# Expert 1 at the fourth position, expert numbers ahead of the tables, logits on four column strips, and the left-over loop behind the last up product

## The chip, the cores and the metric

The kernel runs on one core of one Trainium2 chip. The core has a matrix engine (PE, with its own clock that a throttle grants), a vector engine (DVE), a scalar engine (ACT), GpSimd (POOL), a queue engine that issues most transfers (SP), and 16 DMA engines that carry them from the memory of the chip (HBM) to on-chip memory. The metric is the device time of one execution in microseconds, median of several.

## The reference

One decoder layer on 256 tokens of width 1024, in float32: two token mixers with gates, a layer norm, and a mixture of 32 experts, of which each token uses four, with a layer norm behind.

```python
    p = h @ w_in[l]
    ...
    h = layer_norm(DEEPNORM_ALPHA * h + merged @ w_out[l], ln_mix_g[l], ln_mix_b[l])
    f = moe_ffn(h, w_router[l], b_router[l], w_up[l], b_up[l], w_down[l], b_down[l])
    h = layer_norm(DEEPNORM_ALPHA * h + f, ln_ffn_g[l], ln_ffn_b[l])
```

The expert part, for an expert e and the tokens x that chose it:

```python
logits = (x @ w_router).astype(jnp.float32) + b_router.astype(jnp.float32)
top_val, top_idx = lax.top_k(logits, TOP_K)
gate = jax.nn.softmax(top_val, axis=-1)
...
gu = xe @ w_up[e] + b_up[e]
g = jnp.minimum(gu[:, :F], SWIGLU_LIMIT)
u = jnp.clip(gu[:, F:], -SWIGLU_LIMIT, SWIGLU_LIMIT)
act = (u + 1.0) * (g * jax.nn.sigmoid(SWIGLU_ALPHA * g))
return act @ w_down[e] + b_down[e]
```

Each expert has 8 MB of up weights and 4 MB of down weights.

## The kernel before

The first stage computes the mixers: products with weights split in a high and a low part (line 497), to 277 us. Its last product gives the residual `acc`; two layer norm statistics and `xn` (DVE, line 572) follow. Then comes the router: `turn_z` transposes `xn` in groups of four 128x128 blocks (line 939), `pick` multiplies with the router's weights (line 949) and finds the four best experts of each token on DVE (lines 951 to 962), two small products give each token its rank within an expert (lines 978 to 981), and `gather` picks an expert's tokens with one-hot matrices (line 611, evacuated by ACT at 619 and DVE at 616). `warm` issues products whose results nobody reads (line 931).

The second stage runs over 32 positions. A position takes an expert and has one, two or three blocks of 32 tokens; 52 blocks in all. Positions 0 and 1 are experts 0 and 1 by decree, the others are ordered by how many tokens chose the expert: `place_counts` ranks the experts, `place_left` counts tokens beyond the blocks, and `place_table` builds for every position the ranks, the gates and the expert's number (`ids`). A position's work is cut into steps a, b (the two halves of the up weights) and d (the down weights), in the order a0 b0 a1 d0 b1 a2 d1 b2 and so on. A step has two half slots of 2 MB; `up_part` issues the products of a half slot (line 652: eight products on four column strips of the array for a block), `down_half` those of a down half (line 679). Behind b come the swiglu (658 to 662), the transposes of its result (669) and of the gate weights (634), behind d the scatter into the sum `yacc` (694).

Weights stand in a ring of five buffers of 4 MB, ten half slots. `load_next`, called as soon as a half slot's products are issued, puts the next load of the list `order` into the queue of SP; SP issues its loads in order, and each waits until PE has read the slot. The expert's number comes into a register of SP (line 181) before its load. The first ten half slots are loaded during the mixer stage: up and down of position 0, up of position 1.

Tokens are gathered for several positions at once: a group holds up to four blocks (positions 0 and 1 are group 0), and its four gathers are dealt out between the products of the steps before, one for each `tick` of a quad, by the list `pend`; what is left of them is issued at once ahead of the a step that needs it.

Behind position 31's b and position 30's d stands a loop over blocks that did not fit (line 1049, `n_left` is zero here), then the last down product, the scatter, the statistics and the output. The two rows of the last norm are spread over partitions by four products (line 784), dealt out with `later`.

Of the kernel before, what the change touches and what calls it, by code (L numbers as in the profile page):

```python
# [7 lines left out]
FT = mybir.dt.float32  # L8
# [9 lines left out]
P = 128  # L18
D = 1024
# [8 lines left out]
WHOLE = range(4, 30)  # L28
RESIDUAL_AT, NORM_AT = (5, 11), 16
W1, W2, W3 = 3, 6, 4  # L30
# [5 lines left out]
SINGLE = (2, 3) + tuple(range(5, 24, 2)) + (27, 30, 31)  # L36
TRIPLE = (8, 14, 20)
N2, N3 = 15, 3
BLOCKS = [1 if p in SINGLE else 3 if p in TRIPLE else 2 for p in range(NE)]
CODES = [100, 101] + [0] * (NE - 2)  # L40
for blocks, lo in ((3, 0), (2, N3), (1, N2)):
    for i, p in enumerate([p for p in range(2, NE) if BLOCKS[p] == blocks]):
        CODES[p] = lo + i
assert sorted(CODES[2:]) == list(range(NE - 2))
# [10 lines left out]
def tile_kernel(ctx: ExitStack, tc: tile.TileContext, x, ln_in_g, ln_in_b, w_in, gmlp_ln_g, gmlp_ln_b,  # L55
# [37 lines left out]
    lnrow = keep.tile([2 * NC, P], FT, name="lnrow")  # L93
# [66 lines left out]
    expert_at = {0: 0, 1: 1}  # L160
# [48 lines left out]
    sp1 = s1.enter_context(tc.tile_pool(name="s1", bufs=1))  # L209
# [12 lines left out]
    acc = sp1.tile([P, T, D], FT, name="acc")  # L222
# [54 lines left out]
    def constants():  # L277
# [16 lines left out]
                       channel_multiplier=1, **iota)  # L294
        k["onesf"] = keep.tile([2 * NE, P], FT, name="onesf")
# [218 lines left out]
    for i in range(n_pieces):  # L514
# [8 lines left out]
        if i == 0:  # L523
            for t in range(T):
# [174 lines left out]
    ids = sp2.tile([P, NB], I32, name="ids")  # L699
    left = sp2.tile([P, 1], I32, name="left")  # L700
    e4 = sp2.tile([P, NE], FT, name="e4")
    fours = sp2.tile([P, 2], FT, name="fours")
    nc.gpsimd.iota(fours, pattern=[[4, 2]], base=0, channel_multiplier=0, allow_small_or_imprecise_dtypes=True)
    dyn["ids"] = ids
    cm = sp2.tile([NE, 16], FT, name="cm")
    keys = sp2.tile([NE, NE], FT, name="keys")
    perm = sp2.tile([NE, NB], FT, name="perm")
    shift = sp2.tile([NE, NB], FT, name="shift")
    nc.vector.memset(shift[:, :NE], 0.0)

    def place_counts():
        ps = ps_at()
# [4 lines left out]
        count, key, code, cap, over, nl = (cm[:, i:i + 1] for i in range(6))  # L717
# [7 lines left out]
        nc.vector.tensor_scalar(perm[:, :NE], const["code_of"], code, None, op0=OP.is_equal)  # L725

        nc.vector.tensor_scalar(cap, code, N2 - 0.5, 1.0, op0=OP.is_lt, op1=OP.add)
# [6 lines left out]
        nb = sp2.tile([NE, 1], BF, name="nb")  # L734
        nc.vector.tensor_copy(nb, nl)
        return nb

    def place_left(nb):
        ps = ps_at()
# [407 lines left out]
```

## Time and profile before

| | |
|---|---|
| median of 3 runs | 1248.02 us (1247.41 to 1249.36) |
| the profiled execution | 1248.0 us; its span 1246.3 us |
| PE busy | 1123.0 us, 90% |
| DVE busy | 414.9 us, 33% |
| bytes moved by DMA | 451.05 MB, mean 362 GB/s |
| mean granted clock of PE | 0.943 |

The page cuts the span in 40 slices; each digit is a busy share in tenths, and GB/s is what the DMA engines moved in a slice of 31 us:

```profile
PE   5999999998999899899988999887989889999884
...
DMA  9445546665899999999999999999999999999981
GB/s 356 172 141 197 202 161 251 263 269 211 334 383 399 429 432 421 435 428 431 423 429 430 427 428 432 427 429 431 430 429 428 428 430 428 425 431 426 426 368 52
```

A busy engine is not the same as a limit: PE counts as busy while a pipelined product waits for its operands. The span is from the first to the last instruction; the time of the run has 1.7 us more around it.

### The profile page before, as it was taken

Reading aid. Unit: us, or ns where it says so; the run is one execution under the profiler, and the core shown is the slowest. Engines: PE = TensorE matmul, PEld = TensorE weight load, DVE = VectorE, ACT = ScalarE, POOL = GpSimd, SP = SyncE. Lnnn points to the kernel's source line nnn. Section 1 sums busy time; section 2 is a strip of 40 time slices with the busy share of each in tenths; the row PEclk is TensorE's granted clock in tenths of the full one; section 3 lists DMA queues with packets and bytes.
Section 4 is the critical chain, followed back from the end, with each engine's and each line's share of the span. In section 5 each row is a group of like instructions: output and inputs, shape, how many; then the busy total and the mean of one; then the engine's idle time right before and its main releaser. Section 6 shows DMA issues by size and latency. Waiting matters only on the chain. (4 is left out here: it accounts for less than half of the span.)

```text
span 1246.3 us, 21719 instructions
## 1 busy us (share of the span) xinstructions
PE 1123.0 (90%) x9686; PEld 582.7 (47%) x9686; DVE 414.9 (33%) x784; ACT 214.8 (17%) x353; POOL 116.5 (9%) x125
## 2 busy tenths in 40 slices
PE   5999999998999899899988999887989889999884
PEld 4788788875443343434333444334334333433322
DVE  6854646564432222131223132221213122212213
ACT  3545553421110000101000001010101000100010
POOL 5700200000000000010001010000100000000000
PEclk9999999997999898899899999998989999999866
DMA  9445546665899999999999999999999999999981
GB/s 356 172 141 197 202 161 251 263 269 211 334 383 399 429 432 421 435 428 431 423 429 430 427 428 432 427 429 431 430 429 428 428 430 428 425 431 426 426 368 52
DMA packets 43903, 451.05 MB, mean 362 GB/s; under 512 B 2920, under 2 KB 3580, under 8 KB 26016
## 3 DMA queue, kind: packets, MB, share of 16 engines
q1 hardware_dynamic: 43776, 449.63, 86.7%
q8 instruction: 77, 1.26, 0.4%
q14 instruction: 18, 0.15, 0.0%
q10 hardware_dynamic: 32, 0.01, 0.0%
HBM read 448.58 MB, written 1.05 MB: 361 GB/s over the span
## 5 line engine op out<-in xcount | busy, mean ns | idle before, releaser
L652 PE MATMUL mm<-R,hT 128*32 128x512 f32 x3136 | 382.5, 613 | 19.3 <-DMA R<-in_w_up_dram 18.5
L679 PE MATMUL at<-R,actT 128*32 128x256 f32 x3328 | 225.9, 415 | 23.8 <-DMA R<-in_w_down_dram 9.9
L652 PEld LDWEIGHTS mm<-R,hT 128*32 128x32 f32 x3136 | 89.5, 111 | 206.6 <-issue 173.0
L658 DVE TENSOR_SCALAR gg<-mm 64x512 f32<-64x512 f32 x49 | 33.5, 683 | 401.1 <-PE mm L652 401.1
L679 PEld LDWEIGHTS at<-R,actT 128*32 128x32 f32 x3328 | 103.8, 118 | 123.0 <-issue 45.0
L661 POOL TENSOR_TENSOR gg<-gg,sg 64x512 f32<-64x512 f32 x52 | 66.1, 1271 | 860.3 <-ACT sg L659 842.9
L449 DVE TENSOR_TENSOR wlo<-R,whi 128x1024 fp32r<-128x1024 f32 x77 | 107.9, 1410 | 82.7 <-ACT whi L447 82.5
L497 PE MATMUL mm<-whi,hTl 128*128 128x512 f32 x256 | 101.6, 405 | 4.0 <-DVE hTl L269 4.0
L497 PE MATMUL mm<-wlo,hTh 128*128 128x512 f32 x256 | 101.4, 404 | 3.4 <-DVE wlo L449 3.4
L497 PE MATMUL mm<-whi,hTh 128*128 128x512 f32 x256 | 103.0, 411 | 0.0
L447 ACT ACTIVATE whi<-R 128x1024 fp32r<-128x1024 f32 x80 | 84.4, 1057 | 95.8 <-PE mm L497 93.0
L659 ACT ACTIVATE sg<-gg 64x512 f32<-64x512 f32 x52 | 32.8, 630 | 269.7 <-DVE gg L658 247.6
L686 ACT ACTIVATE y<-at 128x256 f32<-128x256 f32 x52 | 19.9, 383 | 331.7 <-PE at L679 331.7
L611 PEld LDWEIGHTS tp<-pt,xn 128*128 128x128 f32 x464 | 59.5, 201 | 33.3 <-DVE hT L616 22.1
L611 PE MATMUL tp<-pt,xn 128*128 128x128 f32 (+2 forms) x464 | 69.8, 296 | 0.0
L619 ACT ACTIVATE hT<-tp,lm 128x128 f32<-128x128 f32 (+2 forms) x58 | 25.7, 442 | 214.6 <-PE tp L611 214.6
L694 PE MATMUL ac<-y,qt 32*128 32x256 f32 x832 | 60.5, 405 | 0.5 <-ACT y L686 0.5
L671 DVE COPY actT<-tp 128x256 f32<-128x256 f32 x52 | 22.1, 425 | 109.0 <-PE tp L669 108.9
L497 PEld LDWEIGHTS mm<-wlo,hTh 128*128 128x128 f32 x256 | 49.0, 192 | 16.5 <-DVE wlo L449 5.1
L497 PEld LDWEIGHTS mm<-whi,hTl 128*128 128x128 f32 x256 | 48.8, 191 | 16.2 <-DVE hTl L269 5.1
L694 PEld LDWEIGHTS ac<-y,qt 32*128 32x128 f32 x832 | 38.1, 186 | 36.0 <-issue 33.7
L497 PEld LDWEIGHTS mm<-whi,hTh 128*128 128x128 f32 x256 | 49.0, 193 | 11.8 <-ACT hTh L266 0.9
(260 smaller groups left out, 821.8 us busy)
## 6 DMA issues: line engine op xcount, KB each, us to landing
R<-in_w_up_dram SPq DMA_DIRECT2D x52, 4096.0 KB, 38.7
R<-in_w_down_dram SPq DMA_DIRECT2D x26, 4096.0 KB, 33.6
R<-in_w_up_dram SPq DMA_DIRECT2D x24, 2048.0 KB, 8.5
R<-in_w_in_dram SPq DMA_DIRECT2D x13, 2048.0 KB, 9.0
R<-in_w_down_dram SPq DMA_DIRECT2D x11, 2048.0 KB, 10.5
R<-in_w_branch_a_dram SPq DMA_DIRECT2D x2, 2048.0 KB
R<-in_w_branch_b_dram SPq DMA_DIRECT2D x2, 2048.0 KB
R<-in_w_out_dram SPq DMA_DIRECT2D x2, 2048.0 KB
```

Source lines behind the costliest of these rows:

```text
L447: nc.scalar.activation(hi, w, AF.Copy)
L449: eng.tensor_tensor(lo, w, hi.bitcast(FT), op=OP.subtract)
L497: nc.tensor.matmul(ps[t], (a_l if k == 1 else a_h)[:, c, t * P:(t + 1) * P], (lo if k == 2 else hi)[:, cc], start=c == 0 and k == 0, stop= ...
L611: nc.tensor.matmul(ps[:, i * w:(i + 1) * w], zn[:, t, c * P:(c + 1) * P], pt[:, t, :w], start=t == 0, stop=t == T - 1)
L619: nc.scalar.activation(dst[:, c, :w], ps[:, i * w:(i + 1) * w], AF.Identity, scale=lm[:, 0, c:c + 1], bias=lm[:, 1, c:c + 1])
L652: nc.tensor.matmul(ps[n * CAP:(n + 1) * CAP], xs[:, c], w[:, o:o + 512], start=False, stop=c == NC - 1)
L658: nc.vector.tensor_scalar(gg, ps[:2 * CAP], LIMIT, None, op0=OP.min)
L659: nc.scalar.activation(sg, gg, AF.Sigmoid, scale=SW_ALPHA)
L661: nc.gpsimd.tensor_tensor(gg, gg, sg, op=OP.mult)
L671: nc.vector.tensor_copy(at, ps[:, :8 * CAP].rearrange("p (c h s) -> p c h s", c=4, h=2))
L679: nc.tensor.matmul(py[n * CAP:(n + 1) * CAP, :256], at[:, c, h], w[:, o:o + 256], start=h == 0 and c == 0, stop=h == 1 and c == 3)
L694: nc.tensor.matmul(to[n // 2][:, n % 2, t * 256:(t + 1) * 256], qt[s, t], y[s], start=start and t == 0, stop=stop and t == T - 1)
```

## The change

- Expert 1 moves from position 1 to position 3; the ten half slots loaded ahead are now up and down of position 0 and up of position 3. Positions 1 and 2 have one block each. Group 0 holds position 0 alone, group 1 positions 1 to 3.
- The table is cut in three: `place_counts` and `place_ids` give the numbers of the experts between the first up products; `first_table` gives ranks and gates of the positions; `place_caps` and `left_table` the left-over blocks, behind position 5.
- The row matrix of expert 0's bias is a constant made at the start; `acc` and `lnrow` live in the mixer's pool.
- The logits: the router's weights are now the standing operand, 32 columns on one of four strips of the array, and the transposed tokens the moving one, two products for each strip; ACT copies the result, and one more product with `stack` (four identity blocks) sums the strips and turns it.
- The gates are computed behind the first gathers; `warm` issues 4 and 2 products in place of 6 and 4.
- The loop over left-over blocks stands behind the last up product of position 31, ahead of its swiglu and of both last down products; the spreads of the last norm are issued at once behind position 30's b.

```diff
-WHOLE = range(4, 30)
-RESIDUAL_AT, NORM_AT = (5, 11), 16
-W1, W2, W3 = 3, 6, 4
+WHOLE = range(5, 30)
+LEFT_AT, RESIDUAL_AT, NORM_AT = 5, (7, 12), 17
+W1, W2, W3 = 3, 4, 2
...
+STATIC = {0: 0, 3: 1}
+SINGLE = (1, 2, 4, 6, 8, 10, 14, 16, 18, 20, 22, 25, 28, 30, 31)
...
-    order = [(p, k + h) for k, p in steps for h in "01"]
-    i = order.index((2, "a0"))
-    order[i:i + 4] = order[i + 2:i + 4] + order[i:i + 2]
+    uses = [(p, k) for k, p in steps]
+    heads = [(0, "a"), (0, "b"), (0, "d"), (3, "a"), (3, "b")]
+    order = [(p, k + h) for p, k in heads + [u for u in uses if u not in heads] for h in "01"]
...
+        nc.vector.tensor_scalar(rows0, k["rows"], 0.0, None, op0=OP.is_equal)
+
+        k["stack"] = keep.tile([P, NE], FT, name="stack")
+        nc.vector.tensor_copy(k["stack"], ident[:, :NE])
+        for n in range(1, 4):
+            nc.vector.tensor_tensor(k["stack"], k["stack"], ident[:, n * NE:(n + 1) * NE], op=OP.add)
...
+    def place_ids(ps):
+        at = ps[:, 512:512 + NE]
+        nc.tensor.matmul(at, iota_p[:NE].to_broadcast([NE, P]), perm[:, :NE], start=True, stop=True)
+        nc.vector.tensor_copy(ids, at)
+        nc.vector.tensor_scalar(e4, at, 4.0, None, op0=OP.mult)
...
-    groups = [[0, 1]]
-    for p in range(2, NE):
-        if p == 2 or sum(BLOCKS[q] for q in groups[-1]) + BLOCKS[p] > GRP:
+    groups = [[0]]
+    for p in range(1, NE):
+        if p == 1 or sum(BLOCKS[q] for q in groups[-1]) + BLOCKS[p] > GRP:
...
                 up_part([u], 3)
+                if u == LAST:
+                    left_blocks()
                 end_up(u)
...
+    def logits(t, ps):
+        for c in range(NC):
+            n = c % 4
+            nc.tensor.matmul(ps[n * NE:(n + 1) * NE, :P], wrg[:, c], hT2[:, c, t * P:(t + 1) * P], start=c < 4, stop=c >= 4)
+        lt = sp2.tile([P, T, P], FT, name="ptg", bufs=2)[:, 0]
+        nc.scalar.activation(lt, ps[:, :P], AF.Copy)
+        nc.tensor.matmul(ps[:, P:P + NE], lt, const["stack"], start=True, stop=True)
...
+    masks(0)
+    counts = place_counts()
     warm(W3, idle)
     gather_group(0, range(2))
+    start_up((0, 1))
+    first = [(0, 0), (0, 1)]
+    up_part(first[:1], 0)
+    place_ids(counts)
+    up_part(first[1:], 0)
+    gather_group(0, range(2, 4))
...
-                            later(1, lambda a=a, j=j: last_norm(a, j))
+                            last_norm(a, j)
```

The order on SP's queue, behind the last loads ahead of the router. R_69, R_70, R_68, R_67 and R_1944 (R_1951 now) are the five buffers; a row of 128x4096 is a half slot. Before:

```order
L203 DMA R_1944<-in_w_up_dram 128x4096 x2
L972 DMA tables<-in_b_down_dram 32x1024
L973 DMA tables<-in_ln_mix_b_dram 1x1024
L203 DMA R_69<-in_w_down_dram 128x4096 x2
L181 TENSOR_LOAD ids
```

And now:

```order
L206 DMA R_1951<-in_w_up_dram 128x4096 x2
L1036 DMA tables<-in_b_down_dram 32x1024
L1037 DMA tables<-in_ln_mix_b_dram 1x1024
L184 TENSOR_LOAD ids
L184 ISA x2
L206 ISA
L206 DMA R_69<-in_w_up_dram 128x4096
```

The load of an expert's number now stands ahead of the first load into a released slot, where expert 1's down weights, with a fixed number, stood.

The order on PE behind the last up products of position 0 (R_70), to position 1's up products and position 0's down products. `pt`, `xn` are a gather, `act` and `ptg` the transposes, `bup_h` the bias. Before:

```order
L652 MATMUL mm<-R_68,hT_1947 32x512 x4
L611 MATMUL tp<-pt,xn 128x128 x4
L679 MATMUL at<-R_67,actT 32x256 x8
L611 MATMUL tp<-pt,xn 128x128 x4
L679 MATMUL at<-R_67,actT 32x256 x8
L611 MATMUL tp<-pt,xn 128x128 x4
L679 MATMUL at<-R_67,actT 32x256 x8
L611 MATMUL tp<-pt,xn 128x128 x4
L679 MATMUL at<-R_67,actT 32x256 x24
```

And now:

```order
L660 MATMUL mm<-R_70,hT_1954 32x512 x20
L677 MATMUL tp<-ident,act 128x64 x8
L642 MATMUL tp<-ident,ptg 128x128 x4
L619 MATMUL tp<-pt,xn 128x128 x16
L653 MATMUL mm<-bup_h,rows 128x512
L654 MATMUL mm<-bup_l,rows 128x512
L660 MATMUL mm<-R_69,hT_1954 32x512 x4
L619 MATMUL tp<-pt,xn 128x128 x4
L660 MATMUL mm<-R_69,hT_1954 32x512 x4
L619 MATMUL tp<-pt,xn 128x128 x4
```

Group 1's gathers stand in one row ahead of position 1's first up product (R_69), where before they stood between the down products of position 0 (R_67); those of group 2 stand between position 1's up products.

The order on PE at the end. The rows of the loop's body are left out. Before:

```order
L679 MATMUL at<-R_1944,actT 32x256 x16
L669 MATMUL tp<-ident,act 128x64 x4
L634 MATMUL tp<-ident,ptg 128x128 x2
L694 MATMUL ac<-y,qt 128x256 x8
L1048 TENSOR_LOAD left
L1049 COMPARE_AND_BRANCH
...
L1049 UNCONDITIONAL_BRANCH
L679 MATMUL at<-R_70,actT 32x256 x32
L694 MATMUL ac<-y,qt 128x256 x8
```

And now:

```order
L660 MATMUL mm<-R_67,hT_1954 32x512 x8
L917 TENSOR_LOAD left
L918 COMPARE_AND_BRANCH
...
L918 UNCONDITIONAL_BRANCH
L687 MATMUL at<-R_69,actT 32x256 x32
L677 MATMUL tp<-ident,act 128x64 x4
L642 MATMUL tp<-ident,ptg 128x128 x2
L702 MATMUL ac<-y,qt 128x256 x8
L687 MATMUL at<-R_1951,actT 32x256 x32
L702 MATMUL ac<-y,qt 128x256 x8
```

Position 30's down product, its scatter and position 31's transposes have moved from ahead of the loop to behind it. The last branch of the loop carries waits for the eight load queues and for every engine, in both kernels.

## Rows read from the trace of the kernel before

**Rows 1.** The view of stretches: one row for each stretch of the span in us, with its length, the busy time of every engine (and its instructions), PE's granted clock, the busy share of the 16 DMA engines and GB/s.

```profile
core 0: us, PE busy (x) PEld busy (x) DVE busy (x) ACT busy (x) POOL busy (x), PEclk, DMA share, GB/s
360.00:380.00 20.00, 18.96 (x232) 10.62 (x228) 4.73 (x16) 2.60 (x6) 0.00 (x0) 1.00 0.93 384
380.00:400.00 20.00, 18.52 (x192) 7.16 (x188) 5.87 (x12) 1.64 (x3) 2.54 (x2) 1.00 0.98 418
1180.00:1197.00 17.00, 13.45 (x138) 4.57 (x134) 2.48 (x4) 1.01 (x2) 1.26 (x1) 0.98 1.01 428
...
1217.00:1219.00 2.00, 2.00 (x20) 0.92 (x12) 0.00 (x0) 0.38 (x1) 0.00 (x0) 0.50 0.20 80
1219.00:1220.00 1.00, 0.48 (x3) 0.30 (x3) 0.42 (x1) 0.00 (x1) 0.00 (x0) 0.50 0.00 0
1227.00:1230.40 3.40, 3.15 (x32) 1.54 (x36) 0.00 (x0) 0.00 (x0) 0.00 (x0) 0.50 0.00 0
1230.40:1236.00 5.60, 3.21 (x56) 1.60 (x48) 1.78 (x7) 0.38 (x1) 0.00 (x0) 1.00 0.00 0
```

**Rows 2.** The DMA view of 300 to 360 us: a bar of 40 slices of 1.5 us (tenths of the DMA engines' time), the bytes of the stretch, and the up loads issued in it with KB each and median us from issue to landing.

```profile
DMA  0007599999800999989899998994008799999999
...
DMA packets 1270, 18.64 MB, mean 311 GB/s; under 512 B 130, under 2 KB 130, under 8 KB 132
...
R<-in_w_up_dram SPq DMA_DIRECT2D x7, 2048.0 KB, 7.2
```

**Rows 3.** The timeline of SP's queue, 246 to 400 us: start, length, the line that issues, what is loaded, how many loads in the run.

```profile
304.66 3.78 SPq L203 DMA_DIRECT2D R<-in_w_down_dram  x2
318.70 2.13 SPq L203 DMA_DIRECT2D R<-in_w_up_dram  x2
...
328.55 19.47 SPq L203 DMA_DIRECT2D R<-in_w_up_dram  x4
```

**Rows 4.** The timeline of PE, 1160 us to the end: start, busy us, line, operation, out<-in with shapes, instruction records, and in brackets the idle time ahead of it with what ended it.

```profile
1170.01 6.50 PE L679 MATMUL at<-R,actT 128*32 128x256 f32 x64 [2.83 <-DMA R<-in_w_down_dram]
...
1201.31 2.07 PE L784 MATMUL tp<-tables,onesf 1*128 1x512 f32 x2
1203.31 1.94 PE L652 MATMUL mm<-R,hT 128*32 128x512 f32 x8
...
1214.91 3.64 PE L679 MATMUL at<-R,actT 128*32 128x256 f32 x32
1218.48 0.74 PE L669 MATMUL tp<-ident,act 64*128 64x64 f32 x4
...
1220.36 2.09 PE L694 MATMUL ac<-y,qt 32*128 32x256 f32 x16
1227.25 5.21 PE L679 MATMUL at<-R,actT 128*32 128x256 f32 x64 [4.80 <-issue]
```

**Rows 5.** The view of line 1049, the loop: the sequencers' instructions, count, durations in ns as least/median/most, first and last start.

```profile
L1049 PEldq EVENT_SEMAPHORE  x9: 51/51/51, 1222.5 to 1226.9; - x9
...
L1049 PEldq COMPARE_BRANCH  x3: 101/192/3354, 1221.1 to 1227.0; - x3
```

**Rows 6.** The timeline of PE from the mixer's last product to the first up product, columns as in rows 4.

```profile
283.21 0.80 PE L645 MATMUL mm<-bup_h,rows 128*128 128x512 f32 x1 [5.20 <-DVE rows L641]
...
288.13 0.75 PE L939 MATMUL ac<-ident,xn 128*128 128x128 f32 x4
288.71 1.87 PE L949 MATMUL ac<-wr,hT 128*128 128x32 f32 x16
290.96 2.85 PE L949 MATMUL ac<-wr,hT 128*128 128x32 f32 x16 [0.38 <-DVE lg L951]
...
300.86 1.92 PE L652 MATMUL mm<-R,hT 128*32 128x512 f32 x16
```

**Rows 7.** The timeline of DVE around the router, and of the last swiglu of the kernel, columns as in rows 4.

```profile
280.18 2.85 DVE L572 TENSOR_SCALAR xn<-acc,mv 128x1024 f32<-128x1024 f32 x2 [0.29 <-POOL mv L560]
...
295.13 0.29 DVE L962 TENSOR_REDUCE maskb<-eq 128x32 bf16<-128x128 f32 x1
...
1205.31 0.68 DVE L658 TENSOR_SCALAR gg<-mm 64x512 f32<-64x512 f32 x1 [6.23 <-PE mm L652]
...
1208.09 0.68 DVE L662 SCALAR_TENSOR_TENSOR act<-act,gg 64x512 f32<-64x512 f32 x1 [1.37 <-POOL gg L661]
```

**Rows 8.** The timeline of PE in the first expert, columns as in rows 4.

```profile
312.13 0.30 PE L757 MATMUL tp<-ident,gates 128*33 128x128 f32 x1
...
313.24 1.92 PE L652 MATMUL mm<-R,hT 128*32 128x512 f32 x16
315.09 0.43 PE L769 MATMUL at<-perm,tables 32*128 32x64 f32 x2
...
316.79 3.64 PE L652 MATMUL mm<-R,hT 128*32 128x512 f32 x32
...
323.46 0.47 PE L645 MATMUL mm<-bup_h,rows 128*128 128x512 f32 x1 [2.36 <-DVE act L660]
...
333.62 1.16 PE L611 MATMUL tp<-pt,xn 128*128 128x128 f32 x8
...
335.78 1.16 PE L611 MATMUL tp<-pt,xn 128*128 128x128 f32 x8
...
342.75 1.93 PE L679 MATMUL at<-R,actT 128*32 128x256 f32 x32 [0.50 <-ACT y L686]
```

More of the change, by code (lines that the diff above doesn't have):

```diff
@@ L523, in tile_kernel @@
         if i == 0:
+            acc = sp1.tile([P, T, D], FT, name="acc")
             for t in range(T):
@@ L716, in place_counts @@
             nc.tensor.matmul(ps[:NE, NE:NE + 1], maskb[:, t], ones[:, 0:1], start=t == 0, stop=t == T - 1)
-        count, key, code, cap, over, nl = (cm[:, i:i + 1] for i in range(6))
+        count, key, code = (cm[:, i:i + 1] for i in range(3))
         nc.vector.tensor_copy(count, ps[:NE, NE:NE + 1])
@@ L829, in col @@
     def col(p, t, what):
-        if p < 2:
-            return (rk, gates)[what][:, t, p:p + 1]
+        if p == 0:
+            return (rk, gates)[what][:, t, 0:1]
         return tab[:, what * T + t, p:p + 1]
@@ L893, in weigh, with left_blocks @@
         qts[u] = spread(weighted(lambda t: col(p, t, 0), lambda t: col(p, t, 1), k))
+    def left_blocks():
+        n_left = nc.values_load(left[0:1, 0:1], min_val=0, max_val=NOV)
+        with tc.For_i(0, n_left) as i:
+            cur = sp2.tile([P, 2 * T + 1, 1], FT, name="cur")
+            nc.vector.tensor_copy(cur, tab[:, :, bass.ds(i + NE, 1)])
+            idx = sp2.tile([P, 1], I32, name="idx")
+            nc.vector.tensor_copy(idx, cur[:, 2 * T])
+            e = nc.values_load(idx[0:1, 0:1], engines=[mybir.EngineType.SP], min_val=0, max_val=NE - 1)
+            up_e = wu[bass.ds(e, 1)].rearrange("o p n -> (o p) n")
+            ra, rbb, rd = [R[ring[NE - 1, k] // 2] for k in ("a0", "b0", "a0")]
+            nc.sync.dma_start(ra, up_e[:, 0:8192])
+            nc.sync.dma_start(rbb, up_e[:, 8192:16384])
+            four = sp2.tile([P, 1], FT, name="four")
+            nc.vector.tensor_scalar(four, cur[:, 2 * T], 4.0, None, op0=OP.mult)
+            pt = sp2.tile([P, T, GRP * CAP], FT, name="pt", bufs=2)
+            for t in range(T):
+                one_hot(pt[:, t, :CAP], CAP, cur[:, t])
+            xs = xT[(len(groups) - 1) % 2][:, :, :CAP]
+            gather(pt, xs, CAP)
+            ps = ps_mm()
+            up_bias(ps, bias_rows(four))
+            for c in range(NC):
+                up_quad(ps, (ra if c < 4 else rbb)[:, c // 2 % 2 * 4096:], xs, c)
+            nc.sync.dma_start(rd.rearrange("p (h n) -> p h n", h=2), wd[bass.ds(e, 1)].rearrange("o p h n -> (o p) h n"))
+            at = act_T(swiglu(ps))
+            qt = spread(weighted(lambda t: cur[:, t], lambda t: cur[:, T + t], 0))
+            py = ps_at()
+            for h in range(2):
+                down_half(py, at, rd[:, h * 4096:], h)
+            scatter(y_of(py), qt, yacc, False, False)
     def step(kind, p, free):
@@ L970, in tile_kernel @@
     both = ps_ac()
-    picks = [pick(t, both[:, t * 512:(t + 1) * 512]) for t in range(T)]
+    banks = [both[:, t * 512:(t + 1) * 512] for t in range(T)]
+    for t in range(T):
+        logits(t, banks[t])
+    picks = [pick(t, banks[t]) for t in range(T)]
     nc.sync.dma_start(bd[:NE], b_down[0])
     nc.sync.dma_start(bd[NE:], ln_mix_b)
-    idle = ps_ac()[:, :512]
+    idle = ps_at()
     warm(W2, idle)
     for t in range(T):
-        ps = picks[t][0][:, NE:2 * NE]
+        ps = banks[t][:, 256:256 + NE]
         nc.tensor.matmul(ps, before, maskb[:, t], start=True, stop=t == 0)
@@ L1006, in free @@
         def free(p, k):
-            if len(ring) < len(order) and order[len(ring)][0] > 1:
-                while place_table in [f for _, f in pend]:
-                    pend.pop(0)[1]()
             load_next(ring[p, k])
```

123 lines of the change are left out of this document (47 added, 76 removed).

## The prediction

> **What bounds the kernel now.** I read the strip of 40 slices on the page first: PE, the matrix engine, is 90% busy, but from slice 13 on DMA stands at 9 and GB/s between 421 and 435 until the last two slices. So the span has three stages with different limits, and each part of the change must be priced in its own.
>
> In the expert stage the stretches [rows 1] show a DMA share of 0.98 at 418 GB/s in 380 to 400 us and 1.01 at 428 in 1180 to 1197: the weight stream is the limit, and PE work there is free as long as slots come free in time. A 2 MB half slot takes 2.1 MB / 430 GB/s = 4.88 us of stream.
>
> Between the mixer's last product and the steady stream, the stream has holes. The bar of 1.5 us slices [rows 2] shows nothing from 300 to 304.5, nothing from 316.5 to 319.5, and a hole from about 341 to 345. Ten half slots were preloaded; the next six cross here. The SP queue, which issues every load, says why [rows 3]: 304.66 is the moment when PE releases the first slot, 318.70 the moment when the expert numbers exist. 18.64 MB in 60 us is 43.3 us of stream at 430 GB/s, so 16.7 us are lost, and 1.4 us more in 360 to 380 (share 0.93). Later nothing is lost.
>
> The tail begins when the last piece of the last down matrix lands: the share is 0.20 in 1217 to 1219 and 0.00 in the next microsecond [rows 1]. I call this moment L, about 1219.2. PE finishes expert position 30, then stands idle 4.80 us by "issue" before the last down product at 1227.25 [rows 4]; the line of the loop shows a single branch of 3354 ns on PE's sequencer [rows 5]. That is the loop over left-over blocks, whose body this input never enters. The end, 1246.3, is L + 27.1.
>
> So the time is: the moment the stream becomes continuous, plus bytes that do not change, plus the tail. Only the first and the last can move.
>
> **The front: expert numbers and first slots.** In before, the bias product waits until 283.21 for a DVE result [rows 6], because DVE makes the rows tile behind the two normalised halves, which it works on from 280.18 to 283.03 [rows 7]. With the rows made at the start, bias and warm-up run right behind the last product, and the transposes of the first half can start at 280.18 + 1.43 = 281.6; those of the second follow the second half, 283.0. In before the last of four groups ended at 288.88 (288.13 and 0.75 [rows 6]). At some 0.86 a group, the four end near 285.2: 3.7 us earlier.
>
> The logits then cost 1.87 and 2.85 us [rows 6] for two halves of eight products. For four strips of 128 columns there is no row. Bounds: an up part, also eight products on four strips but 512 columns wide, takes 1.92 us at full clock (16 records at 300.86 [rows 6]), so a quarter, 0.48, at best; 1.87 as in before at worst. To either come a copy by ACT (about 0.5, as a group's transposed copy costs) and one more product (about 0.3, as one of the table's). I take 1.0 + 0.5 + 0.3 a half. PE works in order, so the first logits stand at 285.2 + 1.8 = 287.0, the second at 288.8. The Trainium skill, "TensorE: Matmul & The Clock Gate", in the part on packing small matmuls, measured 2.38 times for three column strips; by that, as an estimate, 1.87 would become 0.8 and the sum fall by 0.4 us. No row of before shows it for this shape.
>
> In before the second mask was ready at 295.42, 1.6 us behind its logits (295.13 + 0.29 [rows 7], against 290.96 + 2.85 [rows 6]); now, with short waits, at 290.8. From there to the first up product it was 5.4 us (300.86). The gathers, the ranks and the masks between are the same, the products for the counts come in, four warm-up products go; I take 5.5: 296.3. The two parts of 1.92 us and the product for the numbers (0.2) end at 299.9: first slot free 4.8 us earlier than 304.66. The expert numbers are copied near 298.5, so SP, which waited for them until 318.70, does not wait here. Bounds for this moment: 297.5 if the clock stays full in the chain, 302.5 if half clock lasts through the first up parts, where 1.92 becomes 3.6.
>
> **The middle: where this gain goes.** Position 0 now is a group of its own, so positions 1 to 3 must be gathered before position 1's up products. In before those four gathers lay between the down quads of position 0, at 2.16 us a cycle (333.62, 335.78) [rows 8], and cost PE little that mattered. Now they stand alone, behind position 0's last up product. I build the new moments from the old durations: part 1 of both blocks behind the second gather pair, 299.9 + 2.0 + 3.7 = 305.6; position 0's gate half slots: 311.7 and, with 1.1 for the turned tables (312.13 to 313.24) and 1.3 for five of the seven products of the table (315.09 to 316.79) [rows 8], 315.3. Then PE waits for the second block's swiglu, 3.5 us from the end of its products (1205.31 to 1208.77 [rows 7]; the row at 323.46 shows PE idle 2.36 for it), and turns two activations and two weights, each with a copy: 322. Four gathers of 2.15: 330.5. Position 1's first half slot with two more gathers between its quads: 334.2; the second 338.5; position 0's down halves, at 1.93 for 32 records (342.75 [rows 8]), 346.0 and 349.
>
> Stream by these moments: a 2 MB load lands 7.2 us after its issue [rows 2], of which 4.88 are stream, so 2.2 pass first. Loads flow 302.1–307.0, 307.8–312.7, 313.9–318.8, 318.8–323.7, then nothing (all slots full) until 336.4, then to 341.3, to 346.2, and from 348.2 on without end. Lost in 300 to 360: 18.9 us, with six half slots carried before the hole closes, as in before. The same model on before's issues (304.66, 308.1, 318.7, 320.5, 328.55, 333.75, 344.74; [rows 3] has the first of each run) loses 17.7. So the change loses 1.2 more here, and spares up to 1.4 in 360 to 380, since position 3 lies preloaded and frees four half slots at once. End of the stream moves by −0.2 to +1.2; I take +0.3. The five microseconds gained at the front are spent waiting for the gathers.
>
> **The tail.** The four spreads of the last norm (about 2.07 us a pair of records at half clock [rows 4]) move ahead of position 31 and lie beside its loads. PE reaches the loop near 1203.4. The way out of the loop waits on the semaphores of all eight load queues on each engine, so PE, DVE, ACT and POOL now stand there until L, and both last down products stand behind it. The 3.35 us branch comes ahead of these waits and is hidden; what remains is the eight waits at 51 ns and a branch, some 0.9 us. Then: down of position 30, 64 records, 5.21 as the one at 1227.25 (half clock at its start, 3.2 us; [rows 1, 4]); act transposes and copy 1.2, weight transposes 0.44, scatter 1.15, down of position 31 at full clock 3.85 (twice the 1.93 at 342.75 [rows 8]; at half clock 32 records took 3.64 at 1214.91). The swiglu of position 31 (3.5) lies beside the first product. Sum: L + 0.9 + 5.2 + 1.2 + 0.4 + 1.2 + 3.9 = L + 12.8, against L + 13.3 in before (1227.25 + 5.21). The rest, 13.8 us, is the same. Tail: −0.5. If PE waits 5.2 us for its clock instead of 3.2, the first product takes 5.9: +0.2.
>
> Of the loop's three branches on PE the row has one at 101 ns, one at 192, one at 3354 [rows 5]. The Trainium skill, "Advanced Engine Details and Errata", under control flow timing, gives about 108 ns for a compare and branch; the trace agrees for one of three. By the page the move hides nothing and the tail stays as summed; by the row it matters which branch is the long one, and that is rival E.
>
> **At the start** DVE gets the stack (four operations of about 0.2) and the rows (0.27). They fall in its wait for x and for POOL; I take 0.1, at most 1.2.
>
> **Sum.** Profiled execution 1248.0 (span 1246.3 plus 1.7 outside), equal to the median 1248.02. 0.1 + 0.3 − 0.5 = −0.1: 1247.9. Two-tenths of a per cent, 2.5 us, is about what this measurement can tell from nothing.
>
> **The rivals.**
> A, faster: the front gain survives. If both evacuations of a gather overlap the next one's products and the clock is full in the chain, the first slot is free at 297.5 and position 1's at 330, and everything behind it starts 4 us earlier: 1243.8. For it: PE work of a gather is only 1.16 of 2.16. Against: one PSUM buffer, shown by the equal cycles.
> B, slower: the low clock lasts. PE stands 16 us in the loop instead of 4.8 and restarts cold. If the granted clock stays 0.50 through both products, they take 6.5 each (as the 64 records at 1170.01), scatter 2.09, transposes and copy 1.9 [rows 4]: 0.9 + 6.5 + 1.9 + 2.1 + 6.5 = L + 17.9, 4.6 more than before: 1252.9. It decides from the point at which the rise comes later than the first product's end. Against: the rise came 3.2 us after PE's restart in before.
> C, slower: the gathers standing alone run at half clock, since PE waits there by turns; each of the eight cycles grows by 1 us (1.16 of work becomes 2.2), of which the evacuation hides half: 4 us, 1251.9.
> E, slower: the long branch comes behind the waits in the new place, when the code behind the loop must still be brought in: +3.3, 1251.2. Against: in before it came ahead of them (4.80 idle, eight short waits last).
> D, faster: the loop's exit does not hold the down products. Then position 30's runs as its pieces land, and 31's ends some 3 us behind L: 10 us gained, 1238. Against: the same exit held PE in before.
>
> **Chances.** Forecast 0.48, A 0.22, B 0.11, C 0.10, E 0.05, D 0.04. The forecast's own range is 1245 to 1250.5. Faster: A, D and 0.04 of the forecast, 0.30; slower: B, C, E, 0.26; same 0.44. For eight in ten I leave out D and the far ends of B and C: 1243.0 to 1252.5.
>
> **What would show it.** First load of position 1 issued near 300; a hole in the stream from about 324 to 336; the four gathers in a row behind the weight transposes; PE idle in the loop from 1203 to L + 0.9; the branch hidden; first down product behind it 5 to 6 us. Wrong if the hole is shorter by 3 us, or if the clock row in the tail stays at 0.50.

## The result: slower by 0.6%

The changed kernel takes 1255.51 us (median of 7 runs, 1252.3 to 1257.9) against 1247.41 for the kernel before; the ratio is 1.0059, 95% interval 1.0045 to 1.0074. The prediction was 1247.9, between 1243.0 and 1252.5: the time lies outside the range, on the side that had 0.26. The profiled execution took 1257.9 us (span 1256.2), the longest of the seven, so sizes read from its trace are some 2 us above the median; another session gave 1257.06 (control, below).

### The profile after

Of the page, the strips of DMA and GB/s in 40 slices, now of 31.4 us:

```profile
DMA  9445556675499999999999999899999999999991
GB/s 372 152 162 182 193 194 252 257 294 213 168 400 430 437 431 430 424 432 431 432 431 429 393 425 392 365 430 431 432 430 436 431 429 428 434 431 428 429 414 58
```

Slice 11 (314 to 345 us) has 168 GB/s where before had 334, and slices 23 to 26, in the middle of the expert stage, have 393, 425, 392 and 365 where before had 427 to 432. These are two losses in two places, and both belong to the stream.

The first, in the DMA view of 300 to 360 us (bar of 1.5 us slices), beside which [rows 2] stands:

```profile
DMA  0079989999699999700000000000789999959899
...
DMA packets 1003, 14.80 MB, mean 247 GB/s; under 512 B 99, under 2 KB 99, under 8 KB 99
```

14.80 MB against 18.64: 3.84 MB less, at 430 GB/s 8.9 us. One long hole, from 325.5 to about 342, takes the place of the second and third short ones; the first, to 303, stays. Before lost 2.7 us of its own in 360 to 400 (384 and 418 GB/s, [rows 1]), which the change does not. So 6.2 us remain in this trace. By the bytes moved by 400 us, three other traces with the same front are 3.9 to 5.2 us behind before (control, second run of experiment 1, experiment 3), so the size changes from run to run.

SP's queue there: the first loads behind the router, and the fifth, which is position 2's first. The columns are those of [rows 3]:

```profile
302.36 5.86 SPq L206 DMA_DIRECT2D R<-in_w_up_dram  x2
```

```profile
341.80 4.64 SPq L206 DMA_DIRECT2D R<-in_w_up_dram  x2
```

And PE from the logits to position 1, which answers to [rows 6] and [rows 8]:

```profile
285.81 1.08 PE L1005 MATMUL ac<-hT,wr 128*32 128x128 f32 x16
...
297.17 2.95 PE L660 MATMUL mm<-R,hT 128*32 128x512 f32 x16
...
325.05 2.08 PE L619 MATMUL tp<-pt,xn 128*128 128x128 f32 x8 [0.52 <-DVE qt L644]
328.12 2.08 PE L619 MATMUL tp<-pt,xn 128*128 128x128 f32 x8 [0.99 <-DVE hT L624]
...
337.13 1.94 PE L660 MATMUL mm<-R,hT 128*32 128x512 f32 x8
```

The chain to the first up product is shorter, as summed (297.17, predicted 296.3), but that product runs largely at the low clock (2.95 instead of 1.92 us), and the four gathers of group 1 take 3.07 us each from start to start, not 2.15: their products take 2.08 instead of 1.16 [rows 8], and PE waits 0.99 for the evacuation before each next one.

The stretches, columns as in [rows 1]:

```profile
317.00:325.00 8.00, 3.08 (x16) 1.69 (x12) 4.82 (x12) 0.63 (x1) 2.69 (x2) 0.67 1.01 432
325.00:336.00 11.00, 7.96 (x32) 7.08 (x33) 1.74 (x5) 1.37 (x3) 0.00 (x0) 0.50 0.00 1
...
360.00:380.00 20.00, 15.28 (x162) 5.82 (x154) 4.77 (x10) 1.42 (x3) 1.27 (x1) 1.00 1.01 429
380.00:400.00 20.00, 19.63 (x212) 7.60 (x216) 3.21 (x9) 0.61 (x3) 1.27 (x1) 1.00 1.01 430
700.00:720.00 20.00, 20.00 (x194) 8.10 (x190) 5.10 (x9) 1.65 (x3) 1.46 (x2) 1.00 0.91 371
720.00:740.00 20.00, 17.56 (x228) 8.03 (x216) 5.32 (x13) 0.82 (x3) 1.09 (x1) 1.00 0.98 419
740.00:760.00 20.00, 16.80 (x144) 9.82 (x148) 5.07 (x15) 2.68 (x6) 1.25 (x1) 0.83 1.02 439
760.00:780.00 20.00, 20.00 (x186) 5.91 (x178) 3.87 (x6) 1.26 (x2) 2.44 (x2) 1.00 0.92 377
780.00:800.00 20.00, 17.43 (x210) 8.53 (x210) 6.51 (x17) 1.40 (x3) 1.40 (x2) 0.91 1.00 415
800.00:820.00 20.00, 19.04 (x198) 7.57 (x186) 3.83 (x9) 1.44 (x3) 1.27 (x1) 1.00 0.79 324
...
1225.00:1229.00 4.00, 0.00 (x0) 0.00 (x0) 0.00 (x0) 0.00 (x0) 0.00 (x0) 0.50 0.44 178
1229.00:1230.00 1.00, 0.00 (x0) 0.00 (x0) 0.00 (x0) 0.00 (x0) 0.00 (x0) 0.50 0.00 0
```

In 325 to 336 the clock is at 0.50 throughout and next to nothing moves (1 GB/s). In 700 to 820 the DMA share is under one in slices where PE is busy 20.00 of 20.00. That alone does not make PE the limit, but SP's loads do: those issued from 690 to 810 us whose landing the trace has land 12.0 to 19.3 us after their issue, where in before they take 36.5 to 39.4. A whole load of 4 MB is 9.8 us of stream at 430 GB/s, so there is hardly a load in hand: SP issues one only when PE frees a slot. The missing shares of the six slices add up to 7.6 us; in bytes, as the first loss was counted, it is more: 391 GB/s in 700 to 820 where 430 could pass, 10.9 us. The last bytes land at about 1229.3, ten us later than before.

The tail, on PE, which answers to [rows 4], and the long branch of the loop, which answers to [rows 5]:

```profile
1212.16 1.92 PE L660 MATMUL mm<-R,hT 128*32 128x512 f32 x16
1230.32 5.71 PE L687 MATMUL at<-R,actT 128*32 128x256 f32 x64 [16.24 <-issue]
...
1238.62 3.66 PE L687 MATMUL at<-R,actT 128*32 128x256 f32 x64
```

```profile
L918 PEldq COMPARE_BRANCH  x3: 101/192/5887, 1212.9 to 1230.1; - x3
```

PE stands in the loop for 16.24 us, leaves it 1.0 us behind the last landing and runs the two down products. From the last landing to the end of the span it is 26.9 us (before 27.1). The branch grew to 5.89 us and is hidden under the wait.

### The profile page after: what moved, and what is told of

It is laid out like the page before. It is cut to its first block, busy times and chain, and to the rows that moved or that the text cites. A ratio compares the mean times of both kernels' runs of the same rounds, so it can differ in the third digit from the quotient of the medians.

```text
span 1256.2 us, 21756 instructions
## 1 busy us (share of the span) xinstructions
PE 1117.4 (89%) x9698; PEld 584.3 (47%) x9698; DVE 414.1 (33%) x788; ACT 215.2 (17%) x355; POOL 116.4 (9%) x124
## 4 chain that ended last, share of the span: by engine, by line
PE 70%; DMA 19%; DVE 7%; ACT 2%; POOL 2%; issue 1%; ACTq 0%; DVEq 0%; SPq 0%; POOLq 0%
PE mm L660 22%; PE mm L504 15%; PE at L687 13%; DMA R<-in_w_up_dram 10%; DMA R<-in_w_down_dram 8%; PE tp L619 5%; PE ac L702 4%; PE tp L677 2%; PE at L660 2%; PE tp L642 1%; DVE wlo L456 1%; PE mm L653 1%; DVE gg L666 1%; POOL gg L669 1%; DVE act L668 1%
## 5 line engine op out<-in xcount | busy, mean ns | idle before, releaser
L687 PE MATMUL at<-R,actT 128*32 128x256 f32 x3328 | 216.6, 403 | 30.0 <-issue 16.2
L619 PEld LDWEIGHTS tp<-pt,xn 128*128 128x128 f32 x464 | 63.3, 212 | 37.1 <-DVE hT L624 24.7
L619 PE MATMUL tp<-pt,xn 128*128 128x128 f32 (+2 forms) x464 | 74.1, 308 | 3.5 <-DVE hT L624 3.0
L677 PEld LDWEIGHTS tp<-ident,act 64*128 64x128 f32 x208 | 28.8, 209 | 57.4 <-issue 23.0
```

Source lines behind the costliest of these rows:

```text
L619: nc.tensor.matmul(ps[:, i * w:(i + 1) * w], zn[:, t, c * P:(c + 1) * P], pt[:, t, :w], start=t == 0, stop=t == T - 1)
L677: nc.tensor.transpose(ps[:, c * 2 * CAP:(c + 1) * 2 * CAP], v[:, c], ident[:2 * CAP, :2 * CAP])
L687: nc.tensor.matmul(py[n * CAP:(n + 1) * CAP, :256], at[:, c, h], w[:, o:o + 256], start=h == 0 and c == 0, stop=h == 1 and c == 3)
```

## The experiments

Twelve runs, in three sessions of four: the numbered experiments 1 to 4; the control, the repairs, the second run of 1 and the loop; and the last four. In each the kernel before ran too (1247.17, 1246.01 and 1247.23 us); ratios are to it.

**1. One block list.** The places of one-block and two-block positions:

```diff
-SINGLE = (1, 2, 4, 6, 8, 10, 14, 16, 18, 20, 22, 25, 28, 30, 31)
+SINGLE = (1, 2, 4, 6, 8, 10, 12, 14, 16, 18, 20, 22, 25, 30, 31)
```

> The changed kernel with one list altered: position 12 gets one block and position 28 two (in the changed kernel 12 has two and 28 one), so one-block and two-block positions alternate from 4 to 19. Theory 1 (the row of two-block positions 11 to 13 with a three-block position 15 behind makes PE the limit in the middle): the DMA share of 700 to 820 us goes back from 0.91, 0.98, 1.02, 0.92, 1.00, 0.79 to about 1.00 in each 20 us, the wait from issue to landing of a 4 MB load there grows from 12 to 19 us to over 20, and the time falls by 3 to 8 us, to about 1250. Rival (a disturbance of that one profiled execution, or the later hole at the start): the time stays at 1255 and the middle is again uneven.

Measured: 1247.54 us, ratio 1.0006 (0.9997 to 1.0015). Most of the loss is gone by one number moved in a list. It ran once more for a trace that can be read:

> The kernel with position 12 at one block and 28 at two once more, for its trace. Theory 1: the time is 1247 to 1248 again; the DMA share in 700 to 820 is about 1.00 throughout, while the hole behind 324 stays and the load of position 2 goes out near 338 to 342. Rival: the middle still dips, and the gain lies in a shorter hole.

Measured: 1247.9 us, ratio 1.0015 (1.0006 to 1.0025). The stretches of this second trace:

```profile
325.00:336.00 11.00, 8.02 (x34) 5.97 (x34) 2.52 (x9) 1.84 (x4) 0.00 (x0) 0.50 0.00 0
700.00:720.00 20.00, 16.55 (x216) 7.90 (x212) 4.89 (x12) 1.40 (x3) 0.44 (x2) 1.00 1.01 431
760.00:780.00 20.00, 17.43 (x205) 8.34 (x201) 4.85 (x14) 0.77 (x2) 0.62 (x1) 0.83 0.99 426
800.00:820.00 20.00, 20.00 (x206) 8.98 (x206) 6.93 (x15) 2.95 (x6) 2.56 (x2) 1.00 1.02 435
```

The hole is still there, as expected: nothing moves in 325 to 336, and the first load of position 2 goes out at 339.69. The dip in the middle is gone, 1.01, 0.99 and 1.02 where it was 0.91, 0.92 and 0.79. PE even has slack in two of the three, and the loads issued from 690 to 810 land after 22.4 to 35.8 us. In the changed kernel positions 11, 12 and 13 have two blocks each, a part of the residual (eight small products and a spread) falls at 12, and position 15 has three blocks. From the first bias product of position 11 to that of 16 (617.2 to 778.6 us) PE is busy 150.3 us; the loads of five positions, 30 half slots of 4.88, are 146.4. In this trace, with position 12 at one block, the same stretch (615.0 to 756.9) has 132.8 us of PE. So the work of PE is longer than its loads there, and the slots that the stream had in hand run out. Theory 1 holds.

**2. Two banks for the gathers.**

```diff
-        gather(pts[g], xT[g % 2], width[g], js, g == 0)
+        gather(pts[g], xT[g % 2], width[g], js, g < 2)
```

> The changed kernel with group 1's gathers using two PSUM banks by turns, as group 0's do. Theory 2 (the four gathers standing alone ahead of position 1, at half clock and with one bank, lengthen the hole in the stream): the cycle of 3.07 us falls to about 2.1, the load issued at 341.8 goes out near 338, the time falls by 3 to 4 us, to about 1251.5. Rival (the hole is set by the swiglu of position 0 and the slots, whatever the gathers take): the issue stays near 341 and the time at 1255.

Measured: 1248.49 us, ratio 1.0011 (1.0001 to 1.0022). PE in the hole, and the stretch of 325 to 336 with two of the middle:

```profile
322.59 1.91 PE L619 MATMUL at<-pt,xn 128*128 128x128 f32 x8
324.30 1.25 PE L619 MATMUL tp<-pt,xn 128*128 128x128 f32 x8
325.50 1.16 PE L619 MATMUL at<-pt,xn 128*128 128x128 f32 x8
326.54 1.16 PE L619 MATMUL tp<-pt,xn 128*128 128x128 f32 x8
```

```profile
325.00:336.00 11.00, 11.00 (x83) 6.49 (x83) 3.71 (x12) 2.74 (x6) 0.00 (x0) 1.00 0.35 127
760.00:780.00 20.00, 18.44 (x152) 6.51 (x148) 10.07 (x22) 1.89 (x3) 3.83 (x3) 0.97 0.97 384
780.00:800.00 20.00, 18.98 (x270) 9.10 (x262) 0.54 (x3) 1.15 (x3) 0.00 (x0) 0.95 0.79 326
```

The second bank does more than expected: without the wait for each evacuation PE works without a break, the clock rises during the second gather (1.00 in 325 to 336), and the cycle falls from 3.07 to 1.7, 1.2 and 1.0. In the four traces with one bank for these gathers the clock of 325 to 336 is 0.50, in the two with two banks 1.00 and 0.76. The load of position 2 goes out at 331.30 instead of 341.80; 19.29 MB move in 300 to 360. Of these 10.5 us the edit does not make 1.75, by which the first load was already earlier (300.61); the second run of experiment 1, with one bank and its first load at 300.22, sent position 2's at 339.69. The time falls by 7 us against the first session's 1255.51. The dip in the middle stays (0.79 in 780 to 800): the two losses are separate. Theory 2 holds, with a larger size.

**3. The loop at its old place** in the changed kernel.

```diff
                 up_part([u], 3)
-                if u == LAST:
-                    left_blocks()
...
-                            last_norm(a, j)
+                            later(1, lambda a=a, j=j: last_norm(a, j))
         while pend:
             pend.pop(0)[1]()
+    left_blocks()
```

> The changed kernel with the left-over loop at its old place (behind position 30's down product) and the four spreads of the last norm dealt out as before. Theory 3 (the move of the loop is worth nothing, as the sum of the prediction had it): from the last landing to the end 27 us as in both kernels, time 1255 within 1.5. Rival (PE standing 16 us in the loop and restarting at half clock costs several us): the time falls by 3 us or more.

Measured: 1250.69 us (1246.72 to 1257.75, 12 runs), ratio 1.0040 (1.0019 to 1.0060). Neither: the runs lie in heaps near 1247, 1250 and 1256. The profiled one (1249.91) has a tail of 27.7 us from the last landing, as theory 3 has it, but less of a dip in the middle (shares of 0.96 and more; 419 GB/s in 700 to 820, against 391 in the changed kernel and 385 in its control, which have the same program up to there). What changed between its runs can't be read from one trace, so this run decides nothing on the loop. It suggests that the size of the dip changes with the run: the stream there is on the edge.

**4. The old places under the new front.** Expert 1 at position 1 again, with the groups, blocks and whole loads of the kernel before; constant rows, strips, early numbers and the moved loop stay.

```diff
-STATIC = {0: 0, 3: 1}
+STATIC = {0: 0, 1: 1}
...
-heads = [(0, "a"), (0, "b"), (0, "d"), (3, "a"), (3, "b")]
+heads = [(0, "a"), (0, "b"), (0, "d"), (1, "a"), (1, "b")]
...
-    groups = [[0]]
+    groups = [[0, 1]]
```

> The changed kernel with expert 1 at position 1 again, group 0 holding positions 0 and 1, and the blocks and whole loads of the kernel before; the new front (constant rows, strips, early expert numbers) and the moved loop stay. Theories 1 and 2 together (the new places cost, the front does not): no gathers ahead of position 1, the hole behind 324 us gone, no loss in the middle, time 1243 to 1247. Rival (the front itself costs): 1250 or more.

Measured: 1235.76 us, ratio 0.9913 (0.9900 to 0.9927): 11 us faster than before, beyond what was expected. The DMA view of 300 to 360 us:

```profile
DMA  8998998979999998999898105698999999999999
...
DMA packets 1506, 22.05 MB, mean 368 GB/s; under 512 B 160, under 2 KB 160, under 8 KB 160
```

22.05 MB against 18.64 in before and 14.80 in the changed kernel. The bar shows one hole of two slices, at 333. So the front, which I had thought to be spent on waiting, is worth 3.4 MB, 7.9 us of stream, when no gathers stand ahead of position 1. The new places cost all of that and more.

**Control and repairs.** The changed kernel once more, in the second session:

> The changed kernel itself once more, beside the others of this call. If its loss is its own and not that of the first session: 1252 to 1258 again, with the hole behind 324 us and the dip of the DMA share between 700 and 820. If the first session was disturbed: 1247 to 1250, as the kernels with one part altered showed, and then each of those gains has to be measured anew.

Measured: 1257.06 us, ratio 1.0079 (1.0052 to 1.0105), with 15.24 MB in 300 to 360, and shares of 0.86, 0.96 and 0.74 in 700 to 720, 760 to 780 and 800 to 820. The loss is the kernel's own. Then three repairs at once, the lists of experiment 1, the banks of 2, and this:

```diff
-            while kind == "a" and j_of[group_of[p]]:
-                pend.pop(0)[1]()
...
+    def need(p, j):
+        g = group_of[p]
+        while j_of[g] and j_of[g][0] <= j:
+            pend.pop(0)[1]()
```

`need(p, i)` stands ahead of each half slot's products.

> The changed kernel with three repairs: position 12 at one block and 28 at two, group 1's gathers on two PSUM banks, and each gather issued only ahead of the up products that read it and not all four ahead of position 1. Theories 1 and 2 (two independent losses, about 6 us and 2 to 8 us): both gone, 1236 to 1241. Rival (the two gains are the same microseconds, since a stream that starts earlier only meets the slow middle earlier): 1246 to 1248.

Measured: 1242.41 us, ratio 0.9965 (0.9950 to 0.9980), 14.6 us below the control: close to the sum of the two gains (9 us below the control in the second run of 1; 7 in experiment 2, by the first session), and a little above the range expected. So the two losses are not the same microseconds. The gathers issued late were no help: two run wholly or mostly at half clock again (1.92 and 1.78 us), the load of position 2 goes out at 331.79, no earlier than in experiment 2, and 17.53 MB move, 1.76 fewer than there. Repaired, the change is faster than before by 0.35%, yet 7 us behind the old places.

**The loop again,** under the old places (the edit is that of experiment 3):

> The kernel with the old places and the new front, with the loop and the spreads of the last norm put back as well. Theory 3 (the move of the loop is worth half a microsecond): 1235.5 to 1237, from the last landing to the end 27 us. Rival (the move gained several us of the 12): 1238 or more; or it cost some: 1233 or less.

Measured: 1231.97 us, ratio 0.9893 (0.9875 to 0.9912), 3.8 us below experiment 4, which ran in another session. In the trace the tail is 22.2 us from the last landing, where theory 3 has 27. To compare the two in one session:

> The kernel with old places, new front and the loop put back, once more beside the three others. 1231.5 to 1234. If the last call's 1232.0 came from the chip or the hour, it moves towards 1235.5.

> The same with the loop moved ahead of both last down products, in the same call. Theory 4 (formed after the last call: at the old place the exit need not wait past the last landing when PE's clock is full in the tail, since position 30's down product is done before that landing; the moved loop always puts both products behind it, 27 us): 3 to 5 us above the kernel with the loop put back, about 1236. Rival (theory 3, the move is worth nothing): within 1 us of it.

Measured: 1232.49 us (1229.36 to 1237.40), ratio 0.9893 (0.9872 to 0.9914), with the loop put back; 1235.07 us (1233.77 to 1235.82), ratio 0.9902 (0.9888 to 0.9917), with it moved. By these intervals alone the two can't be told apart. The traces say more. With the loop put back, in the first of these:

```profile
1196.98 1.93 PE L687 MATMUL at<-R,actT 128*32 128x256 f32 x32 [0.87 <-SPq L918]
...
1200.42 1.15 PE L702 MATMUL ac<-y,qt 32*128 32x256 f32 x16
1208.37 5.46 PE L687 MATMUL at<-R,actT 128*32 128x256 f32 x64 [6.80 <-issue]
```

The clock is at 1.00 in 1190 to 1205, so position 30's down product and scatter are done at 1201.6, ahead of the last landing at 1206.7, and the long branch (5.43 us) runs while the last bytes come in. The last product starts 1.7 us behind them, and the tail is 21.0 us. With the loop moved the landing is the same (1206.7), but both products stand behind it: 26.3 us. In the kernel before the same place gave 27.1: PE's clock was 0.50 from 1197 on, and position 30's scatter ended 3.2 us behind the last landing.

Theory 4 is right in that the old place need not wait past the landing, but the clock is not the whole of it. The six traces with the loop at the old place (us):

| trace | scatter of position 30 ends | last landing | long branch | last product starts | tail |
|---|---|---|---|---|---|
| before | 1222.4 | 1219.2 | 3.35 | 1227.25 | 27.1 |
| experiment 3 | 1224.0 | 1220.5 | 3.85 | 1229.27 | 27.7 |
| late numbers (below) | 1206.3 | 1205.8 | 3.85 | 1211.57 | 24.9 |
| old logits (below) | 1207.4 | 1208.5 | 3.39 | 1212.26 | 24.1 |
| loop back | 1205.6 | 1207.8 | 3.85 | 1210.90 | 22.2 |
| loop back, second run | 1201.6 | 1206.7 | 5.43 | 1208.37 | 21.0 |

In all six the last product starts 1.2 us behind the end of the long branch, which begins 0.2 us behind the scatter, and the landing came before the branch ended. So at the old place PE's own lateness and the branch set the tail, not the landing: the branch that the move hides is exposed here. The row of late numbers has a clock of 0.53 in 1190 to 1205 and still a tail of 24.9. With the loop moved the tail is 26.3 to 27.7 over seven traces.

**Two parts of the front,** each taken out of the kernel with old places and loop put back (sister: 1232.49 us in the same session):

```diff
-            n = c % 4
-            nc.tensor.matmul(ps[n * NE:(n + 1) * NE, :P], wrg[:, c], hT2[:, c, t * P:(t + 1) * P], start=c < 4, stop=c >= 4)
-        lt = sp2.tile([P, T, P], FT, name="ptg", bufs=2)[:, 0]
-        nc.scalar.activation(lt, ps[:, :P], AF.Copy)
-        nc.tensor.matmul(ps[:, P:P + NE], lt, const["stack"], start=True, stop=True)
+            nc.tensor.matmul(ps[:, P:P + NE], hT2[:, c, t * P:(t + 1) * P], wrg[:, c], start=c == 0, stop=c == NC - 1)
```

> Old places, loop back, new front, but the logits as in the kernel before: eight products a half with the tokens standing and 32 columns moving, no copy, no product with the stack. If the strips shorten the chain to the first freed slot: the first load behind the router 0.5 to 2 us later and the time 0.5 to 2 us above its sister. Rival (the copy and the sixth product give back what the strips save): within 0.5 us.

Measured: 1236.14 us, ratio 0.9908 (0.9888 to 0.9928). The first load behind the router goes out at 300.61 instead of 298.69, and the last landing is 1.8 us later (1208.5 against 1206.7). But that first load moves from run to run: in the five traces with strips and the old places it goes out at 297.97 to 299.90. Single traces thus give the strips 0.7 to 2.6 us of stream, and by their intervals the two times can't be told apart.

```diff
-    heads = [(0, "a"), (0, "b"), (0, "d"), (1, "a"), (1, "b")]
+    heads = [(0, "a"), (0, "b"), (0, "d"), (1, "a"), (1, "b"), (1, "d")]
...
-    place_ids(counts)
...
     def first_table():
         place_table(0, NE)
+        nc.vector.tensor_copy(ids, tab[:, 2 * T, :NE])
```

> Old places, loop back, new front, but the expert numbers taken from the table behind position 0's first up products, as in the kernel before, and expert 1's down weights loaded first again. If the early numbers are what the front is worth: the third load waits to about 313, the stream loses 3 to 5 us and the time is 3 to 5 us above its sister. Rival (PE's slots set the early stream, not the numbers): within 1 us.

Measured: 1230.76 us, ratio 0.9874 (0.9857 to 0.9891), the lowest median of all, though not apart from its sister by the intervals. 22.16 MB move in 300 to 360, against 21.87 with early numbers. SP's queue:

```profile
297.97 5.90 SPq L206 DMA_DIRECT2D R<-in_w_down_dram  x2
310.19 15.01 SPq L206 DMA_DIRECT2D R<-in_w_up_dram  x4
```

The third load goes out at 310.19, no later than with early numbers (310.29). With two loads of known number ahead, the table is ready when the third slot is.

So the early numbers are worth nothing that shows here, and the strips a part of the 7.9 us. The rest of the front was not taken out by itself. The traces show where it lies: the first transpose behind the mixer starts at 280.80 (loop put back, second run) and at 285.53 in before, whose bias product waits until 283.21 for the rows [rows 6]; and with the numbers from the smaller table the third load goes out at 310.19, in before at 318.70 [rows 3]. What each is worth is not measured.

## Why the prediction was wrong, and where it was right

**Wrong: "So the time is: the moment the stream becomes continuous, plus bytes that do not change, plus the tail. Only the first and the last can move."** The blocks' places had moved for all positions, and the diff showed the list. I priced it at nothing, since PE work "is free as long as slots come free in time", and did not ask whether they do. Three two-block positions in a row ahead of a three-block one cost 10.9 us of stream in the profiled execution; one number moved in the list takes the time from 1257.06 to 1247.9 us in one session. Neither this step nor the next alone carries the result out of the range: with only the hole left the kernel takes 1247.5 and 1247.9 us, with only the middle left 1248.5. Both together do. That the first of these lies on the forecast is in part luck: its trace is 4.2 us of stream behind before's at 400 us and makes that good thinly over the rest of the stream.

**Wrong in size: "End of the stream moves by −0.2 to +1.2; I take +0.3."** The place and the mechanism were right: group 1's gathers standing alone, a hole while all slots are full. The hole was 6.2 us worse than before's by 400 us. The moment for position 2's load came out 7.6 us late, 341.80 against 334.2. Of that, 3.1 us had arisen before the first gather (325.05, summed as 322): the first up part took 2.95 instead of 1.92, and the first slot was free at 302.36, not 299.9, for which the sum's own terms give 300.3. The four gathers then took 3.07 us each instead of 2.15, at a granted clock of 0.50, and this is the term that failed most, 3.6 us. The rest is one quad of position 1 and most of one gather at the low clock. Rival C named the low clock, at 0.10 and 4 us; the four gathers and the first of the two quads before the slot ran low (1.94), the second did not (1.06). The sum also held that before loses nothing behind 380; by bytes it lost 2.7 us in 360 to 400.

The 2.15 itself was misread. In before a down quad of 1.07 us stood between two gathers, which [rows 8] do not show, so the cycle was 1.16 + 1.07 of work and shows no wait for an evacuation:

```profile
334.71 1.07 PE L679 MATMUL at<-R,actT 128*32 128x256 f32 x16
```

With the wait of 0.99 that the changed kernel shows, a cycle at full clock would be 1.16 + 0.99 = 2.15 (an estimate): the same figure, by luck. For the same reason the equal cycles do not show the single buffer, as rival A's paragraph has it.

**Wrong: "The five microseconds gained at the front are spent waiting for the gathers."** True of the changed kernel, but it hid what the front is worth: 7.9 us of stream under the old places (experiment 4).

**Wrong in part: rival A's worth.** It held that evacuations could overlap the next gather's products; one more bank makes them do so (experiment 2), so it was a matter of a buffer, not of chance.

**Right: the front chain.** First up product predicted 296.3, measured 297.17, though in part because terms cancel: the transposes ended at 283.84 (285.2 summed), a half of the logits took 2.04 us (1.8), and mask to up product 6.1 (5.5). The eight products on four strips took 1.08 us (1.0 taken) at a clock of 0.50, where before had 1.87 at 1.00 and 2.85 at 0.65. The Trainium skill, "TensorE: Matmul & The Clock Gate", in its part on packing small matmuls, has 2.38 times for three column strips; the trace agrees in kind: 1.7 times on the rows as they stand, and 2.9 at the same clock, since with the loop put back (second run) eight took 0.64 us at a clock of 1.00.

**Right: the tail.** PE out of the loop 1.0 us behind the last landing (0.9 predicted), the first product 5.71 (5.2 to 5.9), the whole 26.9 us against 27.1 in before, −0.2 (−0.5 predicted). Rival B did not happen: the clock rose before the first product ended. Rival E did not either: the branch of 5.89 us lies ahead of the waits. Rival D is refuted by the 16.24 us of waiting. On the 108 ns that the Trainium skill gives for a compare and branch ("Advanced Engine Details and Errata", control flow timing) the second trace says what the first did: 101 and 192 ns for two, 5887 for the third. What the sum did not see is that the tail of the old place is no constant: it follows from when PE ends position 30's scatter, and fell to 21.0 us where that lay 5.1 us ahead of the last landing.

The last landing is 10.1 us later than before's, less than hole and middle together. In bytes at 430 GB/s the changed kernel is level with before at 300 us (67.09 MB both), 6.3 us behind at 400, 4.9 at 700, 15.5 at 820 and 13.4 at 1200. The last 3.3 us come back at the end, where both streams run at half rate, before from about 1207 on (190 to 256 GB/s until 1217), the changed kernel only from 1223 (213). Why that stretch is shorter, and why the stream gains thinly elsewhere, is open.

## What to carry to other kernels

Where a stream of loads is the limit, work out the other engine's time for each stretch as long as the slots in hand, not for the whole: a heavy stretch costs even when the mean is below the loads'. Here products that waited for their evacuation in a single bank also ran at half clock, so a second bank was worth more than the overlap. And a synchronising exit belongs where its waits are already met: put it behind work that ends well before the last landing, count the branch that leaves it (3.4 to 6.6 us here), and check at which clock the work ahead of it runs. When a stretch of a cycle is read from a trace, look at what the engine did between its rows.

## What the runs showed that was not expected

- The branch that skips the loop's body is dear on PE alone (at most 66 ns on the other engines), and its time goes with the stream: 4.9 to 6.6 us in the eight traces in which 143 to 416 GB/s moved beside it, 3.35 to 3.85 in the five with under 45. Why is not shown.
- Four gathers with a wait of 0.99 us between them stayed at a granted clock of 0.50 for 11 us; the same four without waits reached 1.00 by the second.
- A kernel at the edge between PE and stream can be uneven: 1246.7 to 1257.8 us over twelve runs of experiment 3, against 1234.8 to 1236.3 over five of experiment 4.
